# Hybrid trunk on one core: the 32-row substitution, the rotary and the squares leave GpSimd, and the planner's prices change

## Chip, cores and metric

The kernel runs as one program on one core of one Trainium2 chip. The metric is the device time of one execution in microseconds (us): the median of 3 runs is 945.61 us (944.95 to 947.06). One further execution was profiled; all rows below are from it.

## What is computed

Two layers over 256 tokens of width 2048, all in float32. Cut to what matters here:

```python
for l in range(DEPTH):                                  # 2
    p = rms_norm(x, norm_w[l]) @ w_in[l]                # 2048 -> 6668 columns
    qa, ka, va, za, ub, zb, qkv_c, b_c, a_c, zc = _split_cols(p)
    # A: 12 query and 4 key heads of 64; norm per head, rotary on the first 16 of 64 columns
    qa = apply_partial_rope(rms_norm(qa, q_norm_w[l]), cos, sin)
    ka = apply_partial_rope(rms_norm(ka, k_norm_w[l]), cos, sin)
    oa = sliding_window_sink_attention(qa, ka, va, sinks[l]) * silu(za)
    # B: GLU, causal depthwise convolution of 31 taps, LayerNorm, swish, pointwise product
    ob = conformer_conv_module(ub, ...) * silu(zb)
    # C: 6 heads of 128; delta rule by chunks: (I + L)^-1 with a triangular L per chunk and head
    oc = rms_norm(gated_deltanet(qkv_c, b_c, a_c, ...), c_onorm_w[l]) * silu(zc)
    x = x + concatenate([oa, ob, oc]) @ w_out[l]
```

## The kernel before

**The trunk.** The two projections stream their weights from HBM in granules of 128 x 1024 numbers. ScalarE rounds a granule to a high part (tile `wh`), VectorE forms the low part (`wl` = `st` - `wh`), and TensorE adds three products per weight tile into an accumulator (`acc`): high by high, low by high, high by low. Activations are split in the same way (`xh`, `xl`; for the output projection `ya`, `yb`, `yc`). There are 276 granules; most of TensorE's time goes into these `acc` products, one layer after the other.

**The branches** are generators that run beside the trunk. In the order of the trunk's blocks: first half of q (`qk` 0), the convolution branch's inputs (`u`, `v`), `va`, then `ck`, `cq`, `cv` for the delta rule, the rest of q and k (`qk` 1), and the gates. Three of the branches' strands matter here:
- C, function `c_keys`: a 32 x 32 triangular inverse by forward substitution, 31 steps of a product (`tmp`) and a subtraction (`sub`), 62 instructions a layer, on GpSimd. Its data go through DRAM before and after (`scry`, `sub`, `scrm`, `ms`). Then the blocks are joined to 64 and 128 rows by small matmuls with copies between them: `p32p`, `u32p`, `p64p`, `u64p`. `c_last` follows with `cz`, `cr`, `co` and the transposes `cot`.
- A, function `a_first`: q and k (`aqs`, `aks`) are scaled by their norms (`arr`) on VectorE, multiplied by the norm weights (`qkw`) and rotated (`rt`, `cs`) on GpSimd, transposed on TensorE (`qkt`), and then six pairs of heads go through `sc`, softmax, `ptp` and `ov`.
- B, function `mixer_b`: 30 taps per channel tile, on VectorE (`bacc`) and, each third one, as a product on ScalarE (`bpr`) that VectorE adds afterwards. Products live in the four `bt` buffers.

**What sets the order.** No engine's queue is written by hand. Every instruction is recorded as a note (`Pace.note`), and `Pace.choose` emits notes one at a time: always the one that could start first by the planner's own clock for each engine, and among equals the one whose task has the lower rank. [...] A trunk matmul is the main line: a branch's matmul is put ahead of it only if its data are there at least `MARGIN` ns before. On the chip each engine then works through its queue strictly in that order. Tasks ask for buffers by name (`mx` banks, `big`, `z` and so on); `drop` gives them back, with the planned time if the name stands in `Pace.let`.

Since all recorded instructions are issued at one line, nearly every row carries the line number L337 (L346 in the changed kernel). Rows are therefore told apart by the names of their tiles.

Of the kernel before, what the change touches and what calls it, by code (L numbers as in the profile page):

```python
# [42 lines left out]
MARGIN = 500.0  # L43
# [31 lines left out]
class Pool_:  # L75
# [5 lines left out]
    def tile(self, shape, dt, tag=None, bufs=None, name=None):  # L81
# [5 lines left out]
        born = 0.0  # L87
        if tag in self.pace.let:
# [22 lines left out]
class Pace:  # L111
# [9 lines left out]
    def __init__(self, **free):  # L121
        self.at = dict.fromkeys("PVSGDQ", 0.0)
        self.free = free
        self.let = {"mx": [], "big": []}
# [4 lines left out]
        self.shape = None  # L129
        self.cur = None  # L130
# [111 lines left out]
    def price(self, key, name, a, k, ins, outs):  # L242
# [71 lines left out]
    def emit(self, n):  # L314
# [4 lines left out]
        if n.name.startswith("dma"):  # L319
# [99 lines left out]
def hybrid_trunk(ctx: ExitStack, tc: tile.TileContext, x, positions, norm_w, w_in, q_norm_w,  # L419
# [3 lines left out]
    pace = Pace(mx=8, big=9, z=2, xt=2, pair=2)  # L423
# [53 lines left out]
    xcs, xat = [], []  # L477

    def load_x(*cols):

        j = len(xat) // 2
        if len(xcs) == j:
            xcs.append(big([P, 2, 512], "xc"))
            pace.free["big"] -= 1
        for c in cols:
# [5 lines left out]
    prm = const.tile([P, 66], F32, name="prm")  # L491
    prow = const.tile([66, P], F32, name="prow")
# [15 lines left out]
    qkw = const.tile([P, 2, DEPTH, DA], F32, name="qkw")  # L508
# [4 lines left out]
    def late_loads():  # L513
# [7 lines left out]
        for r0, a, r in ((32, b_conv_b, 8), (40, b_ln_w, 8), (48, b_ln_b, 8), (56, b_pw_b, 8),  # L521
                         (64, c_onorm_w, 2)):
            G.dma_start(prow[r0:r0 + r, :], a.rearrange("l (k p) -> (l k) p", p=P))
            yield "G"
        for dst, src in ((brow, b_conv_w.rearrange("l k c -> (l k) c")),
                         (qkw[:, 0], q_norm_w.partition_broadcast(P)),
                         (qkw[:, 1], k_norm_w.partition_broadcast(P)),
# [64 lines left out]
    def small_params():  # L592
# [3 lines left out]
        PE.transpose(pt[:, :66], prow[:66, :], ident[:66, :66])  # L596
# [3 lines left out]
        V.tensor_copy(prm[:, 56:66], pt[:, 56:66])  # L600
# [9 lines left out]
        V.tensor_scalar(qkw[:, 0], qkw[:, 0], DA ** -0.5, None, ALU.mult)  # L610
# [188 lines left out]
    def keep_x(l, i, xt):  # L799

        (G if l else Q).dma_start(xscr[i], xt.rearrange("p a t -> p (a t)"))
        sq = mid([P, 2, T], "sq")
        S.activation(sq, xt, AF.Square)
        if l not in ssq:
            ssq[l] = cp.tile([P, 2, T], F32, tag="ssq", bufs=1, name=nm("ssq"))
            G.tensor_copy(ssq[l], sq)
        else:
            G.tensor_tensor(ssq[l], ssq[l], sq, ALU.add)
        kept[l] = kept.get(l, 0) + 1

    kept = {}
# [18 lines left out]
    def norm_scale(l):  # L830
        yield lambda: kept.get(l) == KT // 2
        sq = ssq[l][:, 0, :]
        G.tensor_tensor(sq, sq, ssq[l][:, 1, :], ALU.add)
        yield 1
        ps = bank([P, 2], "ssp")
        for tb in range(2):
            PE.matmul(ps[:, tb:tb + 1], sq[:, tb * P:(tb + 1) * P], ones[:, 0:1], start=True,
                      stop=True)
        yield
        m = cmp_([P, 2], "msq")  # L840
        V.tensor_scalar(m, ps, 1.0 / D, EPS, ALU.mult, ALU.add)
        drop()
# [51 lines left out]
    def layer(l):  # L894
# [54 lines left out]
        def c_block(what, i, acc):  # L949
# [5 lines left out]
            if i == 0:  # L955
                if what == "cv":
                    stt["vr"] = big([P, 2, HC, DC], "cvr")
                else:
                    stt[what] = big([P, HC, T], what + "T")
                    stt["ss" + what] = cmp_([P, 2, HC], "ss" + what)  # L960
            dst = z if what == "cv" else stt[what][:, 2 * i:2 * i + 2, :]
# [9 lines left out]
            if what == "cv":  # L971
# [34 lines left out]
        def qk_block(blk, accs):  # L1006
            yield lambda: l in scales
            yield {"big": 1} if "qs" not in stt else None
            rstd = scales[l][0]
            if "qs" not in stt:  # L1010
                stt["qs"] = big([P, 2, HA, DA], "aqs")
                stt["ks"] = mp.tile([P, 2, HKV, DA], F32, tag="ks", bufs=1, name=nm("aks"))
                stt["ssa"] = cmp_([P, 2, HA + HKV], "ssa")
            qs, ks, ssa = stt["qs"], stt["ks"], stt["ssa"]
# [20 lines left out]
        def gate(key, i, acc):  # L1035
# [8 lines left out]
            if "y" + key not in stt:  # L1044
                if key != "b":
                    yield {"big": 2}
                stt["y" + key] = [(bt_ if key == "b" else big)([P, n, T], "y" + key, F32R)
                                  for _ in range(2)]
            yh, yl = stt["y" + key]
# [10 lines left out]
            if 2 * stt["n" + key] == n and key != "b":  # L1060
                drop(1, "big")
# [51 lines left out]
        def out_block(i, acc):  # L1113
# [5 lines left out]
            if l + 1 < DEPTH:  # L1119
# [3 lines left out]
                freed.add(i)  # L1123
# [6 lines left out]
            freed.add(i)  # L1130
# [30 lines left out]
        for i in range(SPLIT):  # L1161
            if i == PWAT:
                pace.until(lambda: "sl" in res)
                sh, sl = res["sh"], res["sl"]
                for j in range(2):
                    acc = channel_block([0, 1, 2, 3], lambda k: (sh[:, k, :], sl[:, k, :]), None,
                                        True, SPLIT + 2)
                    pace.add(0, pointwise(j, acc))
            accs.append(channel_block(FIRST, yact, None, False, SPLIT + 1))
# [6 lines left out]
        drop(4, "big")  # L1176
        if l + 1 == DEPTH:
            pace.until(lambda: not any(pace.lists))

    def mixer_b(l, h, res):  # L1180
# [18 lines left out]
        for g, sa in enumerate(on_act):  # L1199
# [15 lines left out]
        V.tensor_tensor(*done)  # L1215
        s2 = bt_([P, 2, T], "s2")
# [5 lines left out]
        yield  # L1222
        V.tensor_tensor(acc, acc, mu.unsqueeze(1).to_broadcast([P, BT, T]), ALU.subtract)
# [14 lines left out]
        V.tensor_scalar(m, ps, EPS, None, ALU.add)  # L1238
        drop()
# [6 lines left out]
        V.tensor_tensor(acc, acc, row.unsqueeze(1).to_broadcast([P, BT, T]), ALU.mult)  # L1246
        yield
# [102 lines left out]
    def c_keys(l, stt, res):  # L1350
# [461 lines left out]
```

## Time and profile before

| | |
|---|---|
| median of 3 runs | 945.61 us (944.95 to 947.06) |
| the profiled execution | 948.47 us, its span from first to last instruction 946.8 us |
| TensorE matmuls (PE) busy | 915.0 us, 97% of the span |
| weight loads (PEld) busy | 874.3 us, 92% |
| VectorE (DVE) busy | 695.4 us, 73% |
| ScalarE (ACT) busy | 537.8 us, 57% |
| GpSimd (POOL) busy | 211.4 us, 22% |
| mean granted TensorE clock | 0.989 of full speed |
| DMA | 162.20 MB, mean 171 GB/s |

A busy share is an average over stages. TensorE is busy nearly all the time, so what other engines do matters only where TensorE waits for it or where its clock falls. [...]

### The profile page before, as it was taken

To read this page: it belongs to the slowest core of one execution; us is meant where nothing else is said; L and a number is where in the kernel's file an instruction comes from. 1 tells how busy PE (TensorE), PEld (TensorE's weight loads), DVE (VectorE), ACT (ScalarE), POOL (GpSimd) and SP (SyncE) were. 2 spreads that over 40 slices of the span, in tenths; PEclk is the share of its full clock that TensorE was granted. 3 is DMA by queue.
4 is the path that set the end of the run, shared out by engine and by line. 5 is a ranking of instruction groups with operands and counts; after the bars stand their busy time and mean duration, and the time that the engine had idled before them with its cause. 6 is when DMAs were issued, how large, how long until landed. Compare 5 with 4: busy or idle time off the path is not lost.

```text
span 946.8 us, 18260 instructions
## 1 busy us (share of the span) xinstructions
PE 915.0 (97%) x7364; PEld 874.3 (92%) x7364; DVE 695.4 (73%) x1135; ACT 537.8 (57%) x996; POOL 211.4 (22%) x263
## 2 busy tenths in 40 slices
PE   6899999999998999999999999999999999999998
PEld 5799999997898989999989999999879988999998
DVE  6955989999578865547754588999985977654543
ACT  6545895644575764346544379665457567443442
POOL 6500001695056000002310000139803700000000
PEclk9999999999799999999999999999989999999999
DMA  9756545746144435857756655575441542565671
GB/s 297 252 179 183 178 144 183 206 143 194 47 134 134 132 93 159 263 191 252 237 190 179 190 182 166 161 201 179 143 143 50 174 134 90 178 224 186 214 229 39
DMA packets 146068, 162.20 MB, mean 171 GB/s; under 512 B 8063, under 2 KB 129489, under 8 KB 145984
## 3 DMA queue, kind: packets, MB, share of 16 engines
q1 hardware_dynamic: 143808, 155.40, 52.6%
q0 software_dynamic: 2128, 5.62, 2.3%
q8 instruction: 58, 0.95, 0.4%
q14 instruction: 26, 0.21, 0.1%
q10 hardware_dynamic: 48, 0.02, 0.0%
HBM read 152.76 MB, written 8.26 MB: 170 GB/s over the span
## 4 chain that ended last, share of the span: by engine, by line
PE 67%; POOL 14%; issue 8%; DMA 6%; ACT 2%; DVE 2%; SPq 0%; POOLq 0%; ACTq 0%; DVEq 0%
PE acc L337 59%; POOL sub L337 4%; POOL tmp L337 4%; POOL aqs L337 1%; PE ov L337 1%; DMA scrm<-sub 1%; DMA sub<-scry 1%; PE sc L337 1%; DMA xc<-in_x_dram 1%; PE ptp L337 1%; DMA ms<-scrm 1%; POOL rt L337 1%; PE co L337 1%; PE cz L337 1%; POOL ssq L337 1%
## 5 line engine op out<-in xcount | busy, mean ns | idle before, releaser
L337 DVE TENSOR_TENSOR wl<-st,wh 128x1024 fp32r<-128x1024 f32 (+1 forms) x276 | 347.9, 1261 | 176.3 <-ACT wh L337 175.6
L337 ACT ACTIVATE wh<-st 128x1024 fp32r<-128x1024 f32 (+1 forms) x276 | 292.5, 1060 | 264.6 <-PE acc L337 242.6
L337 PE MATMUL acc<-xh,wl 128*128 128x256 f32 x1344 | 381.9, 284 | 0.0
L337 PE MATMUL acc<-xh,wh 128*128 128x256 f32 x1344 | 381.7, 284 | 0.0
L337 PE MATMUL acc<-xl,wh 128*128 128x256 f32 x1344 | 380.5, 283 | 0.0
L337 PEld LDWEIGHTS acc<-xh,wl 128*128 128x128 f32 x1344 | 255.0, 190 | 2.9 <-issue 2.7
L337 PEld LDWEIGHTS acc<-xl,wh 128*128 128x128 f32 x1344 | 253.3, 189 | 2.2 <-issue 2.0
L337 PEld LDWEIGHTS acc<-xh,wh 128*128 128x128 f32 x1344 | 253.0, 188 | 1.7 <-issue 1.4
L337 PE MATMUL acc<-wh,xh 128*128 128x512 f32 (+1 forms) x192 | 70.9, 369 | 2.7 <-ACT wh L337 2.7
L337 PE MATMUL acc<-wl,xh 128*128 128x512 f32 (+1 forms) x192 | 71.6, 373 | 1.8 <-DVE wl L337 1.8
L337 DVE SCALAR_TENSOR_TENSOR bacc<-bh,cbt,bacc 128x254 f32<-128x254 f32 (+19 forms) x160 | 71.4, 488 | 0.1
L337 PE MATMUL acc<-wh,xl 128*128 128x512 f32 (+1 forms) x192 | 71.2, 371 | 0.0
L337 PE MATMUL acc<-yc,wh 128*128 128x256 f32 x360 | 65.6, 282 | 0.0
L337 PE MATMUL acc<-ya,wh 128*128 128x256 f32 x360 | 65.5, 282 | 0.0
L337 PEld LDWEIGHTS acc<-ya,wh 128*128 128x128 f32 x360 | 55.1, 188 | 0.0
L337 PEld LDWEIGHTS acc<-yc,wh 128*128 128x128 f32 x360 | 55.1, 188 | 0.0
L337 PE MATMUL acc<-ya,wl 128*128 128x256 f32 x180 | 50.6, 281 | 0.0
L337 PE MATMUL acc<-yc,wl 128*128 128x256 f32 x180 | 50.5, 280 | 0.0
L337 ACT ACTIVATE bpr<-bh,cbt 128x255 f32<-128x255 f32 (+9 forms) x80 | 37.1, 491 | 23.2 <-DVE bacc L337 23.2
L337 DVE SCALAR_TENSOR_TENSOR ca<-z,cct,ca 128x255 f32<-128x255 f32 (+2 forms) x108 | 48.6, 505 | 0.0
L337 POOL TENSOR_SCALAR_AFFINE_SELECT k<-k 128x768 f32<-128x768 f32 x2 | 2.1, 1067 | 197.5 <-ACT k L337 197.5
L337 PEld LDWEIGHTS acc<-wh,xh 128*128 128x128 f32 x192 | 36.8, 192 | 7.8 <-ACT wh L337 3.1
(302 smaller groups left out, 1359.5 us busy)
## 6 DMA issues: line engine op xcount, KB each, us to landing
st<-in_w_in_dram SPq DMA_DIRECT2D x102, 1024.0 KB, 5.3
st<-in_w_out_dram SPq DMA_DIRECT2D x16, 768.0 KB, 5.1
st<-in_w_out_dram SPq DMA_DIRECT2D x10, 1024.0 KB, 5.4
st<-in_w_out_dram SPq DMA_DIRECT2D x12, 512.0 KB, 3.8
st<-in_w_out_dram SPq DMA_DIRECT2D x16, 256.0 KB, 5.3
st<-in_w_in_dram SPq DMA_DIRECT2D x4, 512.0 KB, 8.5
xscr<-xt SPq DMA_DIRECT2D x8, 256.0 KB, 8.8
xt<-xscr SPq DMA_DIRECT2D x8, 256.0 KB, 4.8
```

What stands on the lines that cost most here:

```text
L337: n.f(*n.a, **n.k)
```

## The change

- `c_keys`: the 62 substitution instructions of a layer go from GpSimd to VectorE, without the pauses every five steps.
- `a_first`: the rotary goes to VectorE. The norm weights are no longer multiplied in: for the first 16 columns they are multiplied into the cosines and sines (`rw`), for the other 48 they are the scale of the copies after the transposes (`prm` columns 64 to 67, loaded by four more small DMAs).
- Sums of squares for the first norm: ScalarE squares the loaded rows of x (`xc`) and sums along the row in the same instruction (`ssx`), so that GpSimd's additions and two small matmuls (`ssp`) go. For the second layer VectorE adds the squares.
- The planner: `MARGIN` from 500 to 800 ns; a table load on ScalarE has a price (1283 ns); `pow` on GpSimd is no longer held apart from VectorE; new landing times for small DMAs; the four `bt` buffers are counted and come free at a planned time; some buffers are given back when the plan says that the work is done (`pace.then`), not when it is recorded.

The core of the diff:

```diff
-MARGIN = 500.0
+MARGIN = 800.0
@@ Pool_.tile
+        if tag == "bt":
+            self.pace.free[tag] -= 1
@@ Pace.__init__
-        self.let = {"mx": [], "big": []}
+        self.let = {"mx": [], "big": [], "bt": 4 * [0.0]}
@@ Pace.price
-            cost = (50 if ps else 95) + 0.85 * n + 90 * (len(ins) - 1) + 93 * (len(outs) - 1)
+            want = {AF.Sin: 9, AF.Ln: 5, AF.Tanh: 0, AF.Exp: 0}.get(a[2], self.table)
+            load = 1283.0 if want != self.table else 0.0
+            self.table = want
+            cost = (50 if ps else 95) + 0.85 * n + 90 * (len(ins) - 1) + 93 * (len(outs) - 1) + load
             return cost, cost + 95, 0
         if len(a) > 3 and a[3] == ALU.pow:
-            return 200 + 170.0 * n, 270 + 170.0 * n, 1
+            return 200 + 170.0 * n, 270 + 170.0 * n, 0
@@ Pace.emit
+                if key == "G":
+                    end = start + issue + 5200.0
             else:
-                end = start + issue + (2600.0 if row >= 128 else 2600.0 + size / 240.0)
+                end = start + issue + 2600.0 + max(0.0, (3.6 * math.prod(out.shape[1:]) - 700.0) if row < 128 else 0.0)
@@ keep_x
-            G.tensor_copy(ssq[l], sq)
-            G.tensor_tensor(ssq[l], ssq[l], sq, ALU.add)
+                V.tensor_copy(ssq[l], sq)
+                V.tensor_tensor(ssq[l], ssq[l], sq, ALU.add)
+    def squares():
+        for j in range(4):
+            yield lambda: len(xat) > 2 * j + 1
+            for tb in range(2):
+                sq = mid([P, 512], "sq")
+                S.activation(sq, xcs[j][:, tb], AF.Square, accum_out=ssx[:, tb, j:j + 1])
...
@@ norm_scale, for the first layer
+            V.tensor_reduce(m, ssx, AX.X, ALU.add)
+            V.tensor_scalar(m, m, 1.0 / D, EPS, ALU.mult, ALU.add)
@@ out_block
-                freed.add(i)
+                pace.then(lambda t: freed.add(i))
@@ mixer_b (and at each other place where a bt buffer is done with)
                 V.tensor_tensor(*done)
+                drop(1, "bt")
@@ c_keys
-            if j % 5 == 0:
-                yield "G"
-            G.tensor_tensor(t, yb[:, j, j + 1:].unsqueeze(2).to_broadcast([112, a, b]),
+            V.tensor_tensor(t, yb[:, j, j + 1:].unsqueeze(2).to_broadcast([112, a, b]),
                             mb[:, j, :b].unsqueeze(1).to_broadcast([112, a, b]), ALU.mult)
-            G.tensor_tensor(mb[:, j + 1:, :b], mb[:, j + 1:, :b], t, ALU.subtract)
+            V.tensor_tensor(mb[:, j + 1:, :b], mb[:, j + 1:, :b], t, ALU.subtract)
@@ a_first
-            G.tensor_tensor(ks[:, tb], ks[:, tb],
-                            qkw[:, 1, l].unsqueeze(1).to_broadcast([P, HKV, DA]), ALU.mult)
-            G.tensor_tensor(qs[:, tb], qs[:, tb],
-                            qkw[:, 0, l].unsqueeze(1).to_broadcast([P, HA, DA]), ALU.mult)
+            for j in range(2):
+                V.tensor_tensor(rw[:, j], cs, qkw[:, i, l, 8 * j:8 * j + 8].unsqueeze(1).unsqueeze(1)
+                                .to_broadcast([P, 2, 2, 8]), ALU.mult)
-            G.tensor_tensor(t, x2, sb, ALU.mult)
+            V.tensor_tensor(t, x2, s2, ALU.mult)
...
-                    S.activation(qT[:, i0:i0 + 2, :], ps, AF.Copy)
+                    S.activation(qT[:, i0:i0 + 2, :], ps, AF.Copy, scale=prm[:, 64 + l:65 + l])
```

Where the changed rules put things is seen in the built program. First, the substitution in the first layer. Before, GpSimd's queue (POOL) holds it in one piece behind the load of `sub`:

```order
L337 DMA sub_2035<-scry 48x32x32 x2
L337 TENSOR_TENSOR tmp_2036<-sub_2035 112x31
L337 TENSOR_TENSOR sub_2035<-sub_2035,tmp_2036 112x31
L337 TENSOR_TENSOR tmp_2036<-sub_2035 112x30
L337 TENSOR_TENSOR sub_2035<-sub_2035,tmp_2036 112x30
```

Now it stands in VectorE's queue (DVE), one step at a time between the trunk's casts (`wl`) and the taps of B (`bacc`); the piece is from its second half:

```order
L346 TENSOR_TENSOR wl_2814<-st_2696,wh_2813 128x1024
L346 TENSOR_TENSOR tmp_1995<-sub_1994 112x130
L346 SCALAR_TENSOR_TENSOR bacc_1040<-bh_661,cbt,bacc_1040 128x229
L346 TENSOR_TENSOR sub_1994<-sub_1994,tmp_1995 112x13x10
L346 SCALAR_TENSOR_TENSOR bacc_1040<-bh_661,cbt,bacc_1040 128x229
L346 TENSOR_TENSOR tmp_1995<-sub_1994 112x120
L346 TENSOR_TENSOR bacc_1040<-bacc_1040,bpr_2300 128x4x234
L346 TENSOR_TENSOR wl_2836<-st_2696,wh_2835 128x1024
```

In all, the 62 steps of the first layer lie between the 53rd and the 80th cast, so that a wait or a long step of theirs stands ahead of casts, and the inverse is ready later in the program than before.

Second, ScalarE's queue (ACT) where the inverse goes from 32 to 64 rows. Before, a product of B (`bpr`) stands ahead of a cast and of the copies `un` and `mp` on which `p64p` waits:

```order
L337 ACTIVATE p_408_2839<-p32p_2883 32x384
L337 ACTIVATE p_408_2839<-p32p_2884 32x384
L337 ACTIVATE bpr_2937<-bh_667,cbt 128x228
L337 ACTIVATE wh_2934<-st_2753 128x1024
L337 ACTIVATE mp_419_2929<-m_406_2837 32x12x32 x2
L337 ACTIVATE un_2838<-u32p_2927 32x384
L337 ACTIVATE un_2838<-u32p_2928 32x384
L337 ACTIVATE mp_419_2929<-un_2838 32x12x32
```

Now no `bpr` stands there, all taps being done; behind the copies come those of the attention pairs (`sm`):

```order
L346 ACTIVATE p_463_3319<-p32p_3375 32x384
L346 ACTIVATE p_463_3319<-p32p_3376 32x384
L346 ACTIVATE wh_3440<-st_3122 128x1024
L346 ACTIVATE mp_477_3435<-m_461_3317 32x12x32 x2
L346 ACTIVATE un_3318<-u32p_3433 32x384
L346 ACTIVATE un_3318<-u32p_3434 32x384
L346 ACTIVATE mp_477_3435<-un_3318 32x12x32
L346 ACTIVATE sm_3322<-ptp_3484 128x384
L346 ACTIVATE sm_3323<-ptp_3485 128x384
L346 ACTIVATE mp_477_3435<-p64p_3510 64x384
```

Third, TensorE's queue (PE) at the same place. Before, the inverse was through (`cot`) before the first `qkt` of the attention; now `qkt` and the first `sc` come ahead of `p32p`, and the steps of the inverse and of the first pairs of heads stand close together with little of the trunk (`acc`) between them:

```order
L346 MATMUL p64p_3511<-mp_477_3435,k_206_1338 64x64 x6
L346 MATMUL ov_3515<-sm_3322,va_1171 64x128
L346 MATMUL ov_3515<-sm_3323,va_1171 64x128
...
L346 MATMUL u64p_3545<-mt_3225,mp_477_3435 64x64 x6
L346 MATMUL u64p_3546<-mt_3225,mp_477_3435 64x64 x6
L346 MATMUL ptp_3522<-ident,sm_3331 128x128 x3
L346 MATMUL ptp_3523<-ident,sm_3332 128x128 x3
...
L346 MATMUL acc_3231<-xh_350,wh_3271 128x256
L346 MATMUL cz_3577<-cvr_2387,mt_3225 128x128 x3
```

Between `p64p` and `u64p`, which needs ScalarE's copies of it, there are six `ov`; between `u64p` and `cz` six `ptp`, four `sc` and one `acc`. The second layer has nearly the same order.

## Rows read from the trace of the kernel before

**Rows 1.** The page, busy time, share of span, instructions of TensorE.

```profile
PE 915.0 (97%) x7364; PEld 874.3 (92%) x7364; DVE 695.4 (73%) x1135; ACT 537.8 (57%) x996; POOL 211.4 (22%) x263
```

**Rows 2.** Waits of TensorE, whole span: us in total, times, longest us.

```profile
PE qkt L337 <- POOL aqs L337: 5.1, 2, 2.6
...
PE p64p L337 <- issue: 3.6, 2, 1.8
...
PE tsum L337 <- DVE z L337: 2.3, 2, 1.1
PE tsum L337 <- DVE ckT L337: 2.0, 4, 0.8
PE acc L337 <- DVE wl L337: 1.8, 2, 1.4
PE tsum L337 <- DVE cqT L337: 1.3, 2, 0.7
...
PE otp L337 <- DVE xt L337: 1.1, 2, 0.5
...
PE ssp L337 <- POOL ssq L337: 1.0, 1, 1.0
```

**Rows 3.** Stretches: us, busy PE, PEld, DVE, ACT, POOL, granted clock, DMA share, GB/s.

```profile
243.20:253.50 10.30, 10.30 (x59) 8.93 (x58) 5.79 (x9) 4.35 (x8) 0.00 (x0) 0.50 0.24 85
301.20:304.70 3.50, 3.40 (x16) 3.40 (x17) 1.73 (x2) 1.40 (x4) 0.05 (x1) 0.51 0.67 231
704.00:710.90 6.90, 6.90 (x41) 6.15 (x40) 4.62 (x6) 2.75 (x5) 0.00 (x0) 0.51 0.23 78
160.00:240.00 80.00, 77.76 (x655) 72.55 (x655) 77.69 (x134) 42.46 (x81) 50.62 (x76) 1.00 0.61 178
240.00:280.00 40.00, 38.21 (x278) 35.41 (x277) 25.74 (x44) 26.90 (x67) 10.03 (x5) 0.87 0.26 80
```

**Rows 4.** Timeline of ScalarE ahead of `p64p`: start us, us, engine, instruction.

```profile
238.36 0.49 ACT L337 ACTIVATE bpr<-bh,cbt 128x228 f32<-128x228 f32 x1 [2.90 <-DVE bacc L337]
...
240.77 0.99 ACT L337 ACTIVATE un<-u32p 32x384 f32<-32x384 f32 x2
241.78 0.52 ACT L337 ACTIVATE mp<-un 32x384 f32<-32x384 f32 x1
```

**Rows 5.** Timeline of TensorE: the ends of its waits for `p64p` and `qkt`, first layer.

```profile
242.41 0.76 PE L337 MATMUL p64p<-mp,kk 64*64 64x64 f32 x10 [1.79 <-issue]
...
301.31 0.47 PE L337 MATMUL qkt<-ident,aqs 128*128 128x128 f32 x1 [2.54 <-POOL aqs L337]
```

**Rows 6.** VectorE's groups, 140 to 176 us, ahead of the substitution.

```profile
L337 DVE TENSOR_TENSOR wl<-st,wh 128x1024 fp32r<-128x1024 f32 x11 | 13.4, 1220 | 1.5 <-ACT wh L337 1.5
L337 DVE SCALAR_TENSOR_TENSOR ca<-z,cct,ca 128x255 f32<-128x255 f32 (+2 forms) x18 | 7.5, 478 | 0.0
```

**Rows 7.** The same groups, 176.4 to 221.3 us, beside the substitution.

```profile
L337 DVE TENSOR_TENSOR wl<-st,wh 128x1024 fp32r<-128x1024 f32 x13 | 17.7, 1362 | 0.7 <-ACT wh L337 0.7
L337 DVE SCALAR_TENSOR_TENSOR ca<-z,cct,ca 128x255 f32<-128x255 f32 (+2 forms) x18 | 9.3, 563 | 0.0
```

**Rows 8.** The casts, 285 to 301 us, beside the rotary.

```profile
L337 DVE TENSOR_TENSOR wl<-st,wh 128x1024 fp32r<-128x1024 f32 x5 | 7.6, 1525 | 0.0
```

**Rows 9.** VectorE's small two-operand instructions, whole span.

```profile
L337 DVE TENSOR_TENSOR aks<-aks,arr 128x256 f32<-128x256 f32 x4 | 1.7, 415 | 0.0
...
L337 DVE TENSOR_TENSOR sco<-wro,rq 128x6 f32<-128x6 f32 x4 | 0.7, 163 | 2.9 <-POOL wro L337 2.9
```

**Rows 10.** Timeline of VectorE: a cast and the instruction behind it.

```profile
169.43 1.22 DVE L337 TENSOR_TENSOR wl<-st,wh 128x1024 fp32r<-128x1024 f32 x1
170.57 1.26 DVE L337 SCALAR_TENSOR_TENSOR ca<-z,cct,ca 128x255 f32<-128x255 f32 x3
```

**Rows 11.** Timeline of VectorE in the first stage.

```profile
22.39 4.77 DVE L337 SCALAR_TENSOR_TENSOR xl<-xt,prm,xh 128x256 fp32r<-128x256 f32 x4
...
29.41 1.66 DVE L337 SCALAR_TENSOR_TENSOR xl<-xt,prm,xh 128x256 fp32r<-128x256 f32 x4
```

More of the change, by code (lines that the diff above doesn't have):

```diff
@@ L87, in tile @@
         born = 0.0
+        if tag == "bt":
+            self.pace.free[tag] -= 1
+            assert self.pace.free[tag] >= 0, "no place of bt"
         if tag in self.pace.let:
@@ L422, in hybrid_trunk @@
     nc = tc.nc
-    pace = Pace(mx=8, big=9, z=2, xt=2, pair=2)
+    pace = Pace(mx=8, big=9, z=2, xt=2, pair=2, bt=4)
     Q = Meter(nc.sync, "Q", pace)
@@ L490, in hybrid_trunk @@
     load_x(256)
-    prm = const.tile([P, 66], F32, name="prm")
-    prow = const.tile([66, P], F32, name="prow")
+    prm = const.tile([P, 70], F32, name="prm")
+    prow = const.tile([70, P], F32, name="prow")
+    V.memset(prow[64:68, :], 1.0)
     S.dma_start(prow[0:32], norm_w.rearrange("l (k p) -> (l k) p", p=P))
@@ L801, in keep_x, with done_x, f @@
         (G if l else Q).dma_start(xscr[i], xt.rearrange("p a t -> p (a t)"))
[L802 to L805, printed above, removed]
-            G.tensor_copy(ssq[l], sq)
-        else:
-            G.tensor_tensor(ssq[l], ssq[l], sq, ALU.add)
-        kept[l] = kept.get(l, 0) + 1
+        if l:
+            sq = mid([P, 2, T], "sq")
+            S.activation(sq, xt, AF.Square)
+            if l not in ssq:
+                ssq[l] = cp.tile([P, 2, T], F32, tag="ssq", bufs=1, name=nm("ssq"))
+                V.tensor_copy(ssq[l], sq)
+            else:
+                V.tensor_tensor(ssq[l], ssq[l], sq, ALU.add)
+            kept[l] = kept.get(l, 0) + 1
+    def squares():
[4 more added lines that the diff above has]
+                S.activation(sq, xcs[j][:, tb], AF.Square, accum_out=ssx[:, tb, j:j + 1])
+                if tb:
+                    done_x(j)
+                yield
+        kept[0] = KT // 2
+    def done_x(j):
+        def f(t):
+            cols_left[j] -= 1
+            if not cols_left[j]:
+                pace.free["big"] += 1
+                pace.let["big"].append(t)
+        pace.then(f)
+    ssx = const.tile([P, 2, 4], F32, name="ssx")
     kept = {}
@@ L831, in norm_scale @@
         yield lambda: kept.get(l) == KT // 2
[L832 to L839, printed above, removed]
-        m = cmp_([P, 2], "msq")
-        V.tensor_scalar(m, ps, 1.0 / D, EPS, ALU.mult, ALU.add)
-        drop()
+        m = cmp_([P, 2], "msq")
+        if l:
+            sq = ssq[l][:, 0, :]
+            V.tensor_tensor(sq, sq, ssq[l][:, 1, :], ALU.add)
+            yield 1
+            ps = bank([P, 2], "ssp")
+            for tb in range(2):
+                PE.matmul(ps[:, tb:tb + 1], sq[:, tb * P:(tb + 1) * P], ones[:, 0:1], start=True,
+                          stop=True)
+            yield
+            V.tensor_scalar(m, ps, 1.0 / D, EPS, ALU.mult, ALU.add)
+            drop()
+        else:
+            V.tensor_reduce(m, ssx, AX.X, ALU.add)
+            V.tensor_scalar(m, m, 1.0 / D, EPS, ALU.mult, ALU.add)
         yield
@@ L960, in c_block @@
                     stt["ss" + what] = cmp_([P, 2, HC], "ss" + what)
+            yield lambda: what == "cv" and "vr" in stt or "ss" + what in stt
             dst = z if what == "cv" else stt[what][:, 2 * i:2 * i + 2, :]
@@ L1007, in qk_block @@
             yield lambda: l in scales
-            yield {"big": 1} if "qs" not in stt else None
             rstd = scales[l][0]
-            if "qs" not in stt:
+            if "ks" not in stt:
+                stt["ks"] = None
+                yield {"big": 1}
                 stt["qs"] = big([P, 2, HA, DA], "aqs")
@@ L1059, in gate @@
             stt["n" + key] = stt.get("n" + key, 0) + 1
-            if 2 * stt["n" + key] == n and key != "b":
-                drop(1, "big")
+            if 2 * stt["n" + key] == n:
+                drop(1, "bt" if key == "b" else "big")
         def pointwise(i, acc):
@@ L1129, in out_block @@
                     PE.transpose(ps[:, tb, c, :], xt[:, c, tb * P:(tb + 1) * P], ident)
-            freed.add(i)
+            pace.then(lambda t: freed.add(i))
             yield
@@ L1176, in layer @@
         drop(4, "big")
+        drop(2, "bt")
         if l + 1 == DEPTH:
@@ L1765, in rest @@
                 drop(1, "big")
-            elif i % 3 == 0:
-                drop(1, "xt")
+            else:
+                drop(1, "bt" if i % 3 else "xt")
             yield
@@ L1777, in hybrid_trunk @@
         pace.add(-2, first_x(i))
+    pace.add(0, squares())
     pace.add(-1, stream.loads())
```

62 lines of the change are left out of this document (38 added, 24 removed).

## The prediction, made before the changed kernel ran

> **What bounds the kernel now.** I read the page first: TensorE is busy for 915.0 us of a span of 946.8 [rows 1]. The trunk's products are not changed, so the change can only win what TensorE loses between them: waits, and stretches at the lower clock. It can lose by making new ones. So the second view is the list of TensorE's own waits [rows 2], the third the granted clock by stretches [rows 3], and then, for each wait, the queue of the engine waited for.
>
> Eight waits can be touched by the change; the others, for the first inputs from HBM, can't. `qkt` waits 5.1 us for the rotary on GpSimd, `p64p` 3.6 us for something that the list can't name, `tsum` 2.3 + 2.0 + 1.3 = 5.6 us for VectorE, a trunk product 1.8 us for a cast, `ssp` 1.0 us for the squares and `otp` 1.1 us for a residual sum [rows 2]. That is 18.2 us. [...] In the first layer the wait of `p64p` ends at 242.41 us and the first stretch begins 0.8 us later; the wait of `qkt` ends at 301.31, where the second begins [rows 3, 5]. The third lies where the second layer is at `p64p`. A stretch of 20.7 us at half speed costs at most half of itself, 10.3 us. So the ceiling of the gain is 18.2 + 10.3 = 28.5 us.
>
> **`qkt`.** The GpSimd instructions ahead of it go; VectorE has the rotary instead, and the new order leaves 0.8 us and not 0.5 between ready data and a branch's matmul. I count 4.6 of the 5.1 us as gone. Nothing else is known to be late there: the scores wait for the same transposes.
>
> **`p64p`.** It needs the copies `un` and `mp`, the last of which ends at 241.78 + 0.52 = 242.30 us. ScalarE was idle for 2.90 us before `bpr`, waiting for VectorE to be done with a `bt` buffer, and `un` stood in its queue behind that [rows 4]. The planner did not know that buffers of this name run out; now it does, and the new order of ScalarE has no `bpr` there. I take 2.6 of the 3.6 us, since what stands close together there now (below) may be late on its own.
>
> **`tsum` and the casts.** Beside GpSimd's substitution a cast on VectorE takes 1362 ns and a tap of C's short convolution 563 [rows 7], ahead of it 1220 and 478 [rows 6]. Beside the rotary a cast takes 1525 [rows 8]. In the first stage four `xl` take 4.77 us beside GpSimd's squares and 1.66 later [rows 11]. So two engines that both read on-chip memory hold each other up, and the planner's guess of that is what made VectorE late. With GpSimd's tensor work gone the guess is not needed. I take 3.5 of the 5.6 us for `tsum`, 2.0 of the 1.8 + 1.0 for the cast and `ssp` (whose matmuls go too), and 0.8 of the 1.1 for `otp`.
>
> **What VectorE gets.** No row shows a substitution step on VectorE. The 31 pairs of steps have (31 - j)(j // 2 + 1) columns each, 92 in the mean. Between 163 ns for 6 columns and 415 ns for 256 [rows 9] a line gives 163 + 86 x 1.0 = 250 ns. But the next instruction starts before the last ends: 1.14 us after a cast that takes 1.22 [rows 10], so on the queue 80 ns less, 170 ns. Bounds per layer: 62 x 0.17 = 10.5 us below, 62 x 0.25 = 15.5 above. I take 10.5, since each step stands between other work and seldom waits for its predecessor. The rotary by the same line: 4 instructions of 32 columns, 6 of 64 and 6 of 192, 0.4 + 0.8 + 1.6 = 2.9 us (above: 4.2). Against it stands what GpSimd no longer slows: 13 x 0.142 + 18 x 0.085 = 3.4 us [rows 6, 7] and 5 x 0.305 = 1.5 us [rows 6, 8]. Net 10.5 + 2.9 - 4.9 = 8.5 us more per layer; above 14.8. Between 160 and 240 us VectorE has 80.00 - 77.69 = 2.3 us to spare, between 240 and 280 another 14.3 [rows 3]. So the work fits as long as what gives way is B's taps and not the casts: they are what hides it. If they can't give way, TensorE waits. The squares of the second layer on VectorE, eight of 512 columns, by the same line about 0.6 us each, lie where TensorE has no wait, and cost nothing as long as VectorE is not full there.
>
> [...]
>
> **The clock.** The 3.5 us stretch followed the `qkt` wait: 1.7 us back. Of the other two, half of 17.2, I take a third, 2.9, because the inverse still has short matmuls and copies in turn. Together 4.6.
>
> **What is new.** The inverse, the first pairs and B's end now meet in one place. TensorE does a matmul in 77.76 / 655 = 119 ns [rows 3]; six `ov` cover 0.7 us, while two copies of the size of `un` take 1.0 [rows 4], behind two for `ptp`. There are four such steps a layer (`p64p`, `u64p`, `cz`, `cr`), each short by 0.3 to 0.8 us: about 2 us a layer, 4 in all.
>
> **Sum.** 4.6 + 2.6 + 3.5 + 2.0 + 0.8 + 4.6 = 18.1 gained, 4 lost: 14.1. The profiled execution, 948.47 us (span 946.8 and 1.7 around it), would be 934.4. It lies 2.86 above the median of the runs, so the median becomes **931.5 us**.
>
> **Rivals.**
> *All of it* is won and nothing new appears: 945.6 - 28.5 = 917.1. For it: nearly every wait in the list has a cause that the new prices name. Against: copies and matmuls still take turns in the inverse. Chance 0.14.
> *The crowd.* Where the three strands meet, ScalarE's copies are the pace: `p64p` waits as before, the clock falls as before, and the new waits are 8 and not 4. Then 18.1 - 2.6 - 4.6 - 8 = 2.9 gained: 942.7. For it: the order shows hardly any `acc` between the steps, and TensorE's clock fell after such a wait twice. Against: the wait then had one cause, `bpr`, and it is gone. Chance 0.24.
> *No effect.* The prices miss the chip in other places by as much, and the waits move: 945.6 give or take 1.9, which is 0.2%, about the least that runs of this kernel can tell. For it: branch matmuls are as many as before. Chance 0.08.
> *VectorE becomes the pace* (the slower side). The place is the 27 casts among which the substitution lies. At the upper bound the net addition is 14.8 a layer, 12.5 more than its stage has to spare; if it stands ahead of the casts, TensorE waits 25 us in two layers and the sum is 945.6 - 14.1 + 25 = 956.5. It decides from about 9.4 us a layer on (2.3 to spare and half of 14.1) that can't give way. For it: VectorE idles only 2.3 of 80 us. Against: the taps of B can give way by more than 14 us. Chance 0.12.
> That leaves 0.42 for the forecast.
>
> **Chances and range.** Faster: forecast, all of it and most of the crowd, 0.79. Same: 0.08. Slower: VectorE and a rest of the crowd, 0.13. The range is 917 to 946: down to the ceiling, up to no change, which leaves out VectorE's case and little more. The forecast's own range is 924 to 938.
>
> **What would show it.** GpSimd's busy time falls from 211 to under 80 us. No wait of `qkt`, `ssp` or a `bpr` that holds `un`. Casts at 1.22 us throughout. Steps of `sub` on VectorE at 0.25 us each, started 0.17 after the one before. If it is wrong, then most likely by waits of `acc` for `wl` between the substitution's first and last step, or by a lower clock where `p64p` to `co` stand.

## The result, and the profile after

The changed kernel takes 916.61 us in the median of 4 runs (916.32 to 918.33) against 946.07 us for the kernel before (4 runs, 944.95 to 947.06): a ratio of 0.9693, 95% interval 0.9676 to 0.971, so 29.5 us faster, where 14.1 were forecast. It is almost the time of the rival *All of it* (917.1 us). The span of the profiled execution fell from 946.8 to 914.2 us.

The page's busy line of the kernel after, beside [rows 1] ("x" counts instructions; in the lists below "<-" names what a tile is made from or what a wait was for, and the granted clock is a share of full speed):

```profile
PE 902.5 (99%) x7360; PEld 867.2 (95%) x7360; DVE 686.2 (75%) x1302; ACT 544.6 (60%) x1004; POOL 75.9 (8%) x93
```

GpSimd went from 211 to 76 us, and VectorE, which got the work, is busy for less time than before, not more. TensorE does the same trunk products and is busy for 12.5 us less; at most 10.3 of that is the half clock of [rows 3], which is gone.

TensorE's waits after, the whole list beside [rows 2] (us in total, times, longest us):

```profile
PE pt L346 <- DMA prow<-in_norm_w_dram: 3.9, 1, 3.9
PE acc L346 <- ACT wh L346: 2.7, 1, 2.7
PE ov L346 <- ACT sm L346: 0.6, 2, 0.5
PE acc L346 <- DVE wl L346: 0.5, 1, 0.5
```

The first two rows are for the first inputs. Of the 18.2 us that the prediction counted, 0.5 is left (a cast); the 0.6 at `ov` are new. Windows over the substitution and over the stages with the inverse, beside [rows 3] (us; busy us and count of PE, PEld, DVE, ACT, POOL; granted clock; DMA share; GB/s):

```profile
171.60:257.00 85.40, 85.30 (x618) 80.39 (x617) 85.36 (x196) 45.89 (x76) 10.71 (x4) 1.00 0.55 173
255.00:300.00 45.00, 44.80 (x484) 41.84 (x483) 32.79 (x97) 38.18 (x102) 8.18 (x8) 1.00 0.35 104
700.00:745.00 45.00, 44.26 (x475) 40.74 (x475) 31.82 (x96) 37.60 (x102) 7.47 (x8) 1.00 0.35 104
```

The granted clock is 1.00 of full speed everywhere. In the first row VectorE is busy for 85.36 of 85.40 us, and TensorE still doesn't wait. What stands there on VectorE, grouped by tile over the whole span (duration min/median/max in ns), and a piece of its timeline (start, us):

```profile
L346 DVE TENSOR_TENSOR tmp<-sub x62: 168/262/301, 171.6 to 700.0; 112x126 f32<-112x126 f32 x6, 112x30 f32<-112x30 f32 x4, 112x56 f32<-112x56 f32 x4, 112x78 f32<-112x78 f32 x4
L346 DVE TENSOR_TENSOR wl<-st,wh x276: 1209/1224/1303, 8.0 to 903.3; 128x1024 fp32r<-128x1024 f32 x134, 128x1072 fp32r<-128x1072 f32 x4
```

```profile
232.12 1.22 DVE L346 TENSOR_TENSOR wl<-st,wh 128x1024 fp32r<-128x1024 f32 x1
233.25 0.28 DVE L346 TENSOR_TENSOR sub<-sub,tmp 112x121 f32<-112x121 f32 x1
233.45 0.45 DVE L346 SCALAR_TENSOR_TENSOR bacc<-bh,cbt,bacc 128x227 f32<-128x227 f32 x1
```

A step of 121 columns lasts 0.28 us and the next instruction starts after 0.20. Over all 124 steps the mean duration is 249 ns and the mean time to the next start 165 ns, against 250 and 170 forecast. Casts take 1.22 us beside them, no longer 1.36 [rows 7] or 1.53 [rows 8].

### The profile page after: what moved, and what is told of

Same layout as the page of the kernel before. It is cut to its first block, busy times and chain, and to the rows that moved or that the text cites. A ratio compares the mean times of both kernels' runs of the same rounds, so it can differ in the third digit from the quotient of the medians.

```text
span 914.2 us, 18230 instructions
## 1 busy us (share of the span) xinstructions
PE 902.5 (99%) x7360; PEld 867.2 (95%) x7360; DVE 686.2 (75%) x1302; ACT 544.6 (60%) x1004; POOL 75.9 (8%) x93
## 4 chain that ended last, share of the span: by engine, by line
PE 58%; issue 29%; DVE 3%; DMA 3%; ACT 3%; POOL 2%; SPq 0%; DVEq 0%; POOLq 0%
PE acc L346 51%; DMA sub<-scry 2%; PE ov L346 1%; DVE wl L346 1%; PE sc L346 1%; PE gram L346 1%; ACT junk L346 1%; DMA st<-in_w_in_dram 1%; PE ptp L346 1%; ACT sm L346 1%; DVE bacc L346 1%; DMA scry<-kk 1%; POOL nk L346 0%; DVE ca L346 0%; ACT wh L346 0%
## 5 line engine op out<-in xcount | busy, mean ns | idle before, releaser
L346 DVE TENSOR_TENSOR wl<-st,wh 128x1024 fp32r<-128x1024 f32 (+1 forms) x276 | 337.8, 1224 | 159.3 <-ACT wh L346 158.9
L346 PE MATMUL acc<-wl,xh 128*128 128x512 f32 (+1 forms) x192 | 69.4, 361 | 0.5 <-DVE wl L346 0.5
L346 PE MATMUL acc<-ya,wh 128*128 128x256 f32 x360 | 65.5, 282 | 0.0
L346 DVE SCALAR_TENSOR_TENSOR ca<-z,cct,ca 128x255 f32<-128x255 f32 (+2 forms) x108 | 45.3, 478 | 0.0
L346 PE MATMUL acc<-yb,wh 128*128 128x256 f32 x240 | 43.6, 283 | 0.0
```

What stands on the lines that cost most here:

```text
L346: n.f(*n.a, **n.k)
```

## The experiments

The theory at the start was the prediction's: each wait has its own cause, some of it GpSimd's contention, some the planner's missing prices, and the clock falls behind the long waits. All runs are listed here; the text below takes them in groups. "Waits" is the sum of TensorE's wait list without the rows for the first inputs; "half clock" is the time at about half of the granted clock, read in steps of 0.5 us; both are of one profiled execution, whose own time stands beside them. Each ratio is to the kernel before as it was timed beside that group of runs; its medians there lie between 945.4 and 946.3 us.

| kernel | median us | ratio to before, 95% | profiled us | waits us | half clock us |
|---|---|---|---|---|---|
| before | 946.07 | | 948.47 | 20.2 | 20.5 |
| after | 916.61 | 0.9693 (0.9676 to 0.971) | 916.32 | 1.1 | 0 |
| e1 new prices only | 949.69 | 1.0034 (1.0008 to 1.006) | 946.89 | 20.8 | 20.4 |
| e2 moves only | 929.21 | 0.985 (0.9802 to 0.9899) | 927.02 | 10.1 | 0 |
| e3 substitution back | 941.92 | 0.9964 (0.9944 to 0.9984) | 942.39 | 15.8 | 21.3 |
| e4 rotary back | 928.75 | 0.983 (0.9796 to 0.9863) | 928.95 | 9.9 | 10.4 |
| e5 idle GpSimd load | 938.20 | 0.9911 (0.9877 to 0.9945) | 942.17 | 18.0 | 10.2 |
| e6 as e3, GpSimd priced | 920.96 | 0.9736 (0.9709 to 0.9763) | 919.02 | 0.7 | 0 |
| e7 as e1, GpSimd priced | 923.71 | 0.9769 (0.9744 to 0.9794) | 923.55 | 5.7 | 7.7 |
| e8 `p64p` made late | 939.37 | 0.993 (0.9901 to 0.9959) | 944.73 | 13.4 | 34.1 |
| e9 after, once more | 918.66 | 0.971 (0.9679 to 0.974) | 920.28 | 4.7 | 0 |
| e10 steps doubled | 940.42 | 0.9955 (0.9925 to 0.9984) | 937.13 | 16.4 | 6.8 |
| e11 power priced longer | 919.55 | 0.9723 (0.969 to 0.9756) | 923.15 | 4.9 | 4.1 |
| e12 moves and landing times | 924.29 | 0.9764 (0.9728 to 0.98) | 925.84 | 6.7 | 3.3 |

The table has one regularity: the profiled time less waits less half of the half clock lies between 913.9 and 919.1 us for every kernel, whichever engine does the work, while the profiled times themselves lie 32 us apart. So the two columns account for most of the differences, and the question is what makes them.

**Prices alone, moves alone (e1, e2).** e1 is the kernel before with the new prices, the margin of 800, the count of `bt` slots and the few changed waits between tasks; e2 is the changed kernel without them:

```diff
-MARGIN = 800.0
+MARGIN = 500.0
...
-        if tag == "bt":
-            self.pace.free[tag] -= 1
...
-                if key == "G":
-                    end = start + issue + 5200.0
```

> Only the planner's new prices and its count of slots; substitution, rotary, norm weights and squares stay on GpSimd as in the kernel before. Theory (each wait has its own cause; the clock falls behind the two long ones): the prices take away p64p's wait, 3.9 us of lost starts, and the two half-clock stretches behind it, 6.3 us; qkt's wait, its stretch and most of the tsum waits stay. 946.1 - 10.2 = 936 us (930 to 941). Rival 'the order is all': the prices alone bring nearly everything, 917 to 921. Rival 'the moves are all': 944 to 948.

> Only the moves off GpSimd; margin 500, no price of table loads, no count of bt slots, the old landing times and the old hold of the power as in the kernel before. Theory: qkt's wait with its stretch, 5.4 + 1.7 us, and tsum's, 7 us, are gone; p64p's wait and two half-clock stretches, 10.2 us, stay, and so does some of the small losses: 946.1 - 14 = 932 us (927 to 937). Rival 'the order is all': 944 to 948, as GpSimd's work was off the path. Rival 'the moves are all': 917 to 920.

e1 gained nothing. Three rows of its wait list:

```profile
PE p32p L346 <- DVE m L346: 9.1, 2, 6.1
PE qkt L346 <- POOL aqs L346: 5.7, 2, 2.8
...
PE tsum L346 <- DVE z L346: 3.3, 2, 1.6
```

`p64p` is gone from it, as the count of slots should bring (e2, below, has no such count and only 0.6 us of that wait, so the count is not shown to be what removes it). But the inverse's first matmuls, `p32p`, now come 6.1 and 3.0 us before their data, and the clock falls there as it did at `p64p`: 0.51 from 235.0 to 242.0 us and 0.52 from 696.0 to 699.5. The theory falls with this: a cause was named rightly and removed, and the loss moved one step up the same chain.

e2 lies where it was expected, but by luck: the `p64p` wait and the half clock that were to stay are gone but for 0.6 us, and the `tsum` waits that were to go are 7.9 us. Its VectorE, and TensorE beside it:

```profile
174.82 0.19 DVE L341 TENSOR_TENSOR tmp<-sub 112x31 f32<-112x31 f32 x1 [2.50 <-DMA sub<-scry]
...
176.44 0.69 DVE L341 SCALAR_TENSOR_TENSOR cqT<-th,ca 128x512 f32<-128x512 f32 x1
```

```profile
177.18 0.66 PE L341 MATMUL tsum<-ident,cqT 128*128 128x128 f32 x4 [2.33 <-DVE cqT L341]
```

The first step of the substitution stands on VectorE and waits 2.50 us for its blocks to come back from DRAM. `cqT` is queued behind it, and `tsum` waits for `cqT`. Before, GpSimd did this waiting, 5.75 us in the first layer, and nobody stood behind it. e12 gives e2 the new landing times alone:

```diff
+                if key == "G":
+                    end = start + issue + 5200.0
...
```

> e2 (only the moves) with one of the new prices: the landing times of DMAs. In e2 VectorE stood 2.5 us in each layer at the first step of the substitution, whose blocks were still under way, with cqT queued behind it and tsum waiting for that, where GpSimd had stood before for free. Theory: that wait goes, 929.2 - 5 = 924 us (921 to 926), and the other prices are worth the remaining 7. Rival 'the margin or the slots did it': 928 to 931.

It took 924.29 us, 4.9 less than e2, and its list has 0.4 us for `cqT` in place of 5.0. So the wait that the moves made was taken away by a price that came with them.

**The substitution and the rotary back on GpSimd (e3, e4).**

```diff
-            V.tensor_tensor(t, yb[:, j, j + 1:]...
+            G.tensor_tensor(t, yb[:, j, j + 1:]...
-            V.tensor_tensor(mb[:, j + 1:, :b], ...
+            G.tensor_tensor(mb[:, j + 1:, :b], ...
```

e4 does the same to the six products of the rotary:

```diff
-            V.tensor_tensor(t, x2, s2, ALU.mult)
+            G.tensor_tensor(t, x2, s2, ALU.mult)
...
```

> The changed kernel with only the substitution's 62 instructions a layer back on GpSimd, replanned. Theory: casts beside it are again 1.3 to 1.4 us instead of 1.22, taps 0.56 instead of 0.48, and what the planner guesses of that makes VectorE late: tsum's 7 us and the cast's 1.4 return, 916.6 + 8 = 925 us (920 to 930). Rival 'room on VectorE is what counts': without the 62 steps VectorE is freer, the time is the same or 1 to 3 us lower, 914 to 917.

> The changed kernel with only the rotary's 12 instructions a layer back on GpSimd (the folded norm weights stay), replanned. Theory: qkt waits for GpSimd again, somewhat less since 8 instructions fewer stand in its chain, about 2 us a layer, and the clock falls for some us behind it: 916.6 + 6 = 922.5 us (919 to 926). Rival 'the planner knows GpSimd's times and places qkt later': 916 to 918.

e3 gave back 25 us, three times what was expected, and through `p32p` again:

```profile
PE p32p L346 <- DVE m L346: 11.7, 2, 5.9
...
PE tsum L346 <- DVE z L346: 3.2, 2, 1.6
```

```profile
232.50:243.00 10.50, 7.09 (x88) 5.08 (x90) 7.16 (x13) 3.82 (x7) 0.00 (x0) 0.51 0.18 54
690.00:700.50 10.50, 6.98 (x86) 4.97 (x88) 7.07 (x13) 3.82 (x7) 0.00 (x0) 0.52 0.21 61
```

Two readings were possible: the contention itself, or an order made with too short a price for GpSimd. The planner gives a step of n columns 180 + 1.95 n ns, 359 for the mean of 92. In e3's trace steps of one size, 31 columns, last 325 to 1576 ns, the mean of all steps is 650, and the whole substitution runs from 173.4 to 221.1 us. In e4 `qkt` does not wait at all, so the wait that was expected did not return; its losses lie at `bss` and `p32p` (4.6 and 1.2 us of waits, and the half clock) and are taken up at e9.

**Which of the two (e5, e6, e7).** e6 and e7 change the price in e3 and in e1, to 735 ns for a step of 92 columns:

```diff
-        cost = 180 + (1.95 if n <= 256 else 1.75) * n
+        cost = 450 + 3.1 * n
```

e5 is the changed kernel with its own order on TensorE, VectorE and ScalarE, and an idle GpSimd product issued behind each step of the substitution, whose result nobody reads:

```diff
+    def extra(out, a, b, op):
+        n = math.prod(out.shape[1:])
+        nc.gpsimd.tensor_tensor(dum[:, :n], dum[:, :n], dum[:, :n], ALU.mult)
```

> The changed kernel in its own order on TensorE, VectorE and ScalarE, with 62 idle products a layer added on GpSimd at the places and with the sizes of the substitution's steps; nobody waits for them. Only the contention comes back. Theory 'contention made VectorE late' (the prediction's): casts beside them 1.36 us for 1.22, taps 0.56 for 0.48; VectorE is never idle between 171 and 257 us, so it falls some 5 us behind, tsum and the casts wait again: 916.6 + 8 = 925 us (921 to 930). Rival 'the place of the inverse': what e3 lost was p32p's wait and the clock, because GpSimd's steps take longer than the planner's price; contention alone costs little: 916 to 919.

> e3 (substitution back on GpSimd) with one more change: the planner's price of a GpSimd product raised to about what the trace of e3 shows, 0.45 us and 3.1 ns a column. Rival of before, now the better theory 'the place of the inverse': p32p is put later, its two waits of 6 us and the two half-clock stretches go: 941.9 - 20 = 922 us (918 to 927). Theory 'contention itself': the time stays at 935 to 942.

> e1 (all tensor work on GpSimd, new prices) with the same raised price of a GpSimd product. Theory 'the place': waits of p32p and qkt and most half-clock stretches go, 949.7 - 24 = 926 us (920 to 934), so that pricing alone would have brought most of the gain without any move. Theory 'the moves': GpSimd's durations scatter (0.27 to 1.6 us for like steps), no one price fits, 938 to 950.

e6, with contention and all, has no wait of a branch left to speak of, and its interval overlaps with that of e9:

```profile
PE acc L346 <- DVE wl L346: 0.5, 1, 0.5
...
PE ov L346 <- ACT sm L346: 0.2, 1, 0.2
```

e7 has every tensor instruction on GpSimd, 209.7 us busy, and is 26.0 us faster than e1 by one line of price, on top of e1's other new prices. Its `qkt`, `p32p` and `tsum` don't wait. What it has left is one place in the first stage, where GpSimd adds the squares; TensorE's waits, GpSimd's and VectorE's timelines there, and the window after:

```profile
PE acc L346 <- DVE wl L346: 5.0, 2, 4.5
```

```profile
25.02 6.54 POOL L346 TENSOR_TENSOR ssq<-ssq,sq 128x512 f32<-128x512 f32 x4 [3.23 <-ACT sq L346]
```

```profile
23.33 3.46 DVE L346 SCALAR_TENSOR_TENSOR xl<-xt,prm,xh 128x256 fp32r<-128x256 f32 x6
...
27.32 1.68 DVE L346 TENSOR_TENSOR wl<-st,wh 128x1024 fp32r<-128x1024 f32 x1
```

```profile
26.00:33.00 7.00, 3.95 (x9) 3.15 (x10) 7.00 (x6) 3.34 (x6) 6.69 (x7) 0.52 0.61 192
```

So the substitution can stay on GpSimd, contention and all, for 2.3 us over e9 and 4.4 over after, once the planner gives it more time; that other work is then put where the contention falls is argued and not shown. In the first stage of e7 the longer price did not help. e5 has the contention in an order that doesn't know of it: 938.2 us, 21.6 above after and above what both theories expected. Its wait list:

```profile
PE tsum L361 <- DVE z L361: 5.1, 4, 2.0
PE p32p L361 <- DVE aex L361: 4.6, 1, 4.6
...
PE bss L361 <- DVE bsq L361: 2.8, 2, 1.4
```

From 171 to 210 us C's taps take 554 ns and 476 in the same stretch of after, casts 1243 and 1216. The casts were hit less than [rows 7] would say, the taps as much, and `tsum` waits again as it did before the change. Not all of the 21.6 us is that. Set beside after matmul by matmul, e5's profiled execution ends 25.7 us later: 7.0 of it arise at the `tsum` of both layers, about what the contention was expected to cost, 11.1 between `qkt` and the half clock behind `bss`, in part by the power below, and 6.0 at `p32p` in the second layer and in the half clock there. For the last, e5's GpSimd:

```profile
712.56 13.46 POOL L466 TENSOR_TENSOR dum<-dum 112x91 f32<-112x91 f32 x13
726.35 1.92 POOL L361 DMA_DIRECT2D scrm<-sub  x2 [0.33 <-DVE bacc L361]
```

Thirteen idle products stand in GpSimd's queue behind the power and ahead of the DMA that sends the substitution's result to DRAM. It is issued 5.7 us after VectorE's last step (720.67 us), in after 0.3 us (700.71 and 700.40). So somebody did wait for the idle products, and e5 is not a test of the contention alone.

**Two tests with the order held (e8, e10).** e8 puts four GpSimd copies of `mp` onto itself ahead of `p64p`; e10 adds an idle VectorE product behind each step of the substitution:

```diff
+    def extra(out, *a, **k):
+        for _ in range(4):
+            nc.gpsimd.tensor_copy(out, out)
...
-        S.activation(m64[32:64, :, 0:32], un[32:64], AF.Copy)
+        SX.activation(m64[32:64, :, 0:32], un[32:64], AF.Copy)
```

> The changed kernel in its own order with four copies on GpSimd, about 0.65 us each, put between ScalarE's last copy into mp and p64p, which waits for them: p64p is late by about 1.8 us, twice. Theory 'the clock follows a wait': two half-clock stretches of some 7 to 10 us come back behind p64p: 916.6 + 3.6 + 9 = 929 us (926 to 932). Rival 'the clock followed what stands around p64p before, not the wait': granted clock stays 1.0, 916.6 + 3.6 = 920 us (918 to 922).

> The changed kernel in its own order, with each of the substitution's 62 steps a layer on VectorE followed by an idle product of the same size: some 0.16 us each on the queue, 10 us a layer that the planner doesn't know. Rival of the prediction 'VectorE becomes the pace': VectorE is full from 171 to 257 us, so all of it but a lead of 2 us comes out at TensorE, and the clock falls behind the waits: 916.6 + 16 to 28 = 933 to 945 us. Against it 'the casts run ahead': TensorE's casts are done some us before they are needed, 917 to 922.

e8's waits and the windows behind them:

```profile
PE p64p L361 <- POOL mp L463: 6.9, 2, 4.3
```

```profile
287.00:301.00 14.00, 13.15 (x89) 11.38 (x89) 2.48 (x10) 6.37 (x13) 0.80 (x1) 0.51 0.03 10
744.50:758.50 14.00, 14.00 (x90) 12.00 (x90) 1.76 (x6) 6.52 (x14) 0.00 (x0) 0.51 0.24 76
```

The waits came out at 3.5 us and not 1.8, and behind each the clock stood at about half (0.51 in both windows) for some 13.7 us, where after has 1.00. Set beside after matmul by matmul, the delay grows by 6.9 us at the two `p64p` and by 12.0 more in the stretches behind them. So here the same matmuls ran at half speed when the inverse was entered through a wait of 2.7 or 4.3 us, and at full speed when it was not. What else e8 lost, 10.1 us in this comparison, lies ahead of `p64p`, at `qkt` and `bss`, where nothing was edited (e9), and in a half-clock stretch behind one `bss`.

e10 lost 23.8 us, as the rival *VectorE becomes the pace* would have it: 249 ns of duration and 165 of queue time for each added product, 20 us in all, and these waits.

```profile
PE tsum L361 <- DVE z L361: 5.7, 3, 2.5
PE mu L361 <- DVE s L361: 5.3, 2, 2.7
```

Its casts cost TensorE only 1.3 us. It is the branches' small products that were late, and most of the added time came out at TensorE.

**The power on GpSimd (e9, e11).** In e4, e5 and e8 VectorE stands 3.4 us for `arr`, a power of 32 columns.

e9 is the changed kernel unedited, and e11 has one price changed:

```diff
-            return 200 + 170.0 * n, 270 + 170.0 * n, 0
+            return 200 + 170.0 * n, 270 + 340.0 * n, 0
```

> The changed kernel once more, nothing edited. It settles how to read e4, e5 and e8: there GpSimd's power of 32 columns (arr) takes 10.7 us with VectorE's instructions the same as in the profile of after, where it takes 6.91 (5.42 where VectorE leaves gaps), and VectorE stands 3.4 us behind it, twice. Theory 'GpSimd has to find a gap in VectorE's stream, and which one it finds is decided by tens of ns': either value can come, with 916 to 919 us where it is 6.91 and 922 to 930 where it is 10.7. Rival 'the edits made it long': 6.91 and 916 to 918 again.

> The changed kernel with one price changed: a power on GpSimd is known after 0.34 us a column instead of 0.17, so that the products with arr stand later on VectorE, replanned. Theory 'a gap must be found': no VectorE wait for arr, whether it takes 6.9 or 10.7 us; 913 to 918 us on every chip, and clearly below e9 if there it is 10.7. Rival: the attention's start moves later with it and its matmuls crowd at the end of the stage, 919 to 925.

e9 has both values in one execution of one program. GpSimd in the first and in the second layer, then VectorE in both:

```profile
240.94 6.90 POOL L346 TENSOR_TENSOR arr<-arr,expo 128x32 f32<-128x32 f32 x1 [51.73 <-DVE arr L346]
...
686.24 10.71 POOL L346 TENSOR_TENSOR arr<-arr,expo 128x32 f32<-128x32 f32 x1 [51.73 <-DVE arr L346]
```

```profile
242.44 0.38 DVE L346 TENSOR_TENSOR rw<-cs,qkw 128x32 f32<-128x32 f32 x2
...
246.37 0.68 DVE L346 TENSOR_TENSOR s<-bacc 128x512 f32<-128x512 f32 x1
...
687.73 0.29 DVE L346 TENSOR_TENSOR rw<-cs,qkw 128x32 f32<-128x32 f32 x2
...
691.56 0.75 DVE L346 TENSOR_TENSOR s<-bacc 128x512 f32<-128x512 f32 x1
...
696.98 0.42 DVE L346 TENSOR_TENSOR aks<-aks,arr 128x256 f32<-128x256 f32 x1 [3.39 <-POOL arr L346]
```

Set beside after matmul by matmul, TensorE is 3.1 us later behind that place. This explains the wait at `aks` in e4, e5 and e8 and part of what they show at `qkt` and `bss`; what the rotary on GpSimd costs e4 apart from it was not separated. It takes nothing from the result: e9's four executions took 916.8, 917.0, 920.3 (the one profiled) and 921.0 us, and the lower pair has the time of after. In e11 `aks` stands later. VectorE no longer waits for `arr`, though it took 10.71 us there too, but `p32p` waits 2.2 us and the time is that of e9: about what the rival named for it would give. No version here beats the changed kernel.

## Why the prediction was right, and where it was off

Faster was forecast, and the waits and the half clock that it named are gone. The size was off: twice the forecast gain, and a time 0.4 us under the low end of the range (917), where the prediction had its ceiling of the gain.

**The terms.** What the lists and windows give for each, the clock at its most (half of the 20.7 us, 10.3 + 3.5 + 6.9, in [rows 3]):

| term | forecast us | measured us |
|---|---|---|
| `qkt` | 4.6 | 5.1 |
| `p64p` | 2.6 | 3.6 |
| `tsum` | 3.5 | 5.6 |
| cast and `ssp` | 2.0 | 2.3 |
| `otp` | 0.8 | 1.1 |
| clock | 4.6 | 10.3 |
| new waits | -4.0 | -0.6 (`ov`) |
| sum | 14.1 | 27.4 |

The span fell by 32.6 us, more than the ceiling of 28.5. Counted by starts (a matmul loses what its distance to the next exceeds the median of its tiles and shapes, if more than 30 ns), TensorE lost 65.5 us before and 32.3 after. Of the difference, 20.8 us are losses of 250 ns and more outside the half-clock stretches, 7.8 lie in these stretches, and 4.7 are smaller losses outside them, which hardly show in a list of waits and which the ceiling did not have.

**Where it was off.** With the clock at its most, two terms make 9.1 of the 13.3 us between the sums. *The clock*: the step "Of the other two, half of 17.2, I take a third" discounted stretches for short matmuls in turn with copies. In after these take turns as before, and none of the 20.7 us is left; in e8 they run at half clock again, behind a wait for `p64p`. *What is new*: the step "each short by 0.3 to 0.8 us: about 2 us a layer" counted only the six `ov` as cover. After's ScalarE and TensorE at that place:

```profile
277.48 0.53 ACT L346 ACTIVATE mp<-un 32x384 f32<-32x384 f32 x1
...
279.45 0.48 ACT L346 ACTIVATE mp<-p64p 64x384 f32<-64x384 f32 x1 [0.55 <-PE p64p L346]
280.15 0.48 ACT L346 ACTIVATE mp<-p64p 64x384 f32<-64x384 f32 x1 [0.21 <-PE p64p L346]
```

```profile
278.51 0.91 PE L346 MATMUL p64p<-mp,kk 64*64 64x64 f32 x12
279.26 0.86 PE L346 MATMUL p64p<-mp,k 64*64 64x64 f32 x12
280.05 0.88 PE L346 MATMUL ov<-sm,va 128*64 128x128 f32 x12
280.85 0.33 PE L346 MATMUL u64p<-mt,mp 64*64 64x64 f32 x2
```

The last copy ahead of `p64p` ends at 278.01, and `p64p` starts 0.50 us later with no wait noted. The first copy of its result runs beside the second half of `p64p`, the second beside `ov`, and `u64p` starts 0.2 us after it. None of the four steps stands in the list of waits, only 0.6 us at `ov`. *The crowd* did not come.

*The list of waits*: the step "the others, for the first inputs from HBM, can't" left out three rows of before that are not for first inputs, 2.0 us in all, and are gone after; what removed them was not tried.

```profile
PE otp L337 <- DMA xt<-xscr: 1.2, 1, 1.2
...
PE u32p L337 <- DVE mt L337: 0.6, 2, 0.3
PE p32p L337 <- DVE m L337: 0.2, 1, 0.2
```

*VectorE's load*: the step "Net 10.5 + 2.9 - 4.9 = 8.5 us more per layer" has the wrong sign. VectorE's busy time fell by 9.2 us over the span. The 124 steps add 20.7 us to it, as priced, but the casts (`wl`) take 11.7 us less over the span and `xl` 5.3, and many smaller groups gain too, where the prediction counted relief in two stretches of a layer only.

**What held.** VectorE's price: 250 ns and 170 ns were 249 and 165. So in the mean the next instruction started 84 ns before a step's end. VectorE is full for 85 us without harm (85.36 of 85.40 us busy, TensorE 85.30), and e10 shows that it had no room to spare: 20 us more cost 23.8.

**What was right for a reason only half right.** The prediction laid `qkt` to GpSimd's rotary, and `tsum` and the casts to contention, as if the moves had to come to take them away. What the two engines contend for no run shows, only that a cast took 1362 and 1525 ns beside GpSimd's work [rows 7, 8] and 1220 ahead of it [rows 6]; the planner's guess of it is that some instructions of the two wait for each other in the plan. e7 takes the waits at `qkt` and `tsum` away with all of that work on GpSimd, by a price. `p64p` was laid to the missing count of slots; e1 removes that wait and loses as much at `p32p`, and in e2 all but 0.6 us of it is gone without the count. Most of what the kernel before lost was lost by an order made with times that GpSimd does not keep. e7 gets 22 of the 29.5 us by new prices, a longer one for GpSimd among them, without which (e1) they get nothing; the moves get them by giving the work to an engine whose times the planner knows. The moves' own part, after or e9 against e7, is 5 to 7 us, most of it the squares' place in e7. The folding of the norm weights, the margin, the price of table loads and the count of slots were not tried one by one, nor was the longer price of GpSimd without the other new prices.

## What to carry to other kernels

Where an order is written by a planner, compare its prices with the trace first: one line of price was worth 26 us between e1 and e7, and a move to another engine may only be worth what it does for the planner's knowledge. Look at what stands behind a step that waits for a DMA: in the kernel before it waited 5.75 us on GpSimd and nobody stood behind it, in e2 it waited 2.50 us on VectorE, and `tsum` waited 2.33 us for what was queued behind it. Count the half clock behind a wait with the wait: e8's 6.9 us of waits cost 12.0 more.

## What the runs showed of the hardware

GpSimd's power of 32 columns took 5.42 to 5.43 us in the kernel before, e1, e3, e6 and e7, 6.43 in e2, 6.9 in after, 7.07 in e10, 7.65 in e12 and 10.7 in e4, e5 and e8; e9 and e11 have 6.90 and 10.71 in one execution. In e9 the instruction of VectorE that stands 5.43 us before the power's end is 0.07 to 0.09 us longer than its twin in the other layer (0.38 and 0.29, 0.75 and 0.68). That is what one would see if the power had to be let in between VectorE's instructions and then took 5.43 us; this is argued from the rows and was not tested. VectorE did not stand still for it: in e9's first layer it went on with two-operand instructions all through those 5.43 us, casts of 1.21 us among them.

Not every wait was followed by a lower clock. e2's two `tsum` waits of 2.3 us left it at 1.00, and so did e9's `bss` wait of 1.4 us, while the same wait of 1.4 us in the first layer of e5 and of e8 had half-clock stretches of 6.9 and 6.8 us behind it (0.51 from 275.5 to 282.5 us and from 270.0 to 277.0). In e10 a `tsum` wait of 2.5 us was followed by such a stretch in the first layer and its like in the second was not, and so it was with `qkt`'s two waits of 2.5 and 2.6 us in the kernel before. The waits above 4 us in these runs (4.3 to 6.1) all had one at or behind them.
